# Levels 2 and 3, and level 4 and the pairs, of each head's chain as one run of small products each, from held copies; the sample's small products beside them

## The chip, the cores and the metric

The program runs on one core of a Trainium2 chip. Its time is the device time of one execution in microseconds (us). Before the change it is 2061.63 us, the median of three runs (2060.82 to 2062.42).

## The reference

One layer of a streaming encoder is computed for a prompt of 2048 tokens (width 1024) and for 32 further tokens of a running stream (the sample), with the same weights. Cut to what matters here:

```python
h = rmsnorm(x, g_pre_mix)
z = h @ w_in
u, zq, zf, zi, zg = jnp.split(z, [...], axis=-1)
y_pool = pool_mix(u_ext, n_valid, w_pool, pool_scale)
q = jax.nn.silu(zq)
fgate = lbf + (1.0 - lbf) * jax.nn.sigmoid(zff)
kin = (1.0 - lbf) * jax.nn.sigmoid(-zff)
logf = jnp.log(fgate)
S1, o = hgrn_run(S0, to_heads(q), to_heads(kin), to_heads(zi), to_heads(logf))
o = rmsnorm(o, g_hg_norm)
y_hg = o * jax.nn.silu(zg)
x = x + rmsnorm(jnp.concatenate([y_pool, y_hg], axis=-1) @ w_out, g_post_mix)
h2 = rmsnorm(x, g_pre_ffn)
x = x + rmsnorm((jax.nn.silu(h2 @ w_gate) * (h2 @ w_up)) @ w_down, g_post_ffn)
```

`hgrn_run` is a recurrence with a decay of its own for every token and channel, four heads of 128 channels. Within a chunk it needs, for every pair of tokens s <= t:

```python
b = jnp.cumsum(logf, axis=2)
decay = jnp.exp(jnp.where(causal, b[t] - b[s], -inf))
attn = jnp.einsum('bhtk,bhsk,bhtsk->bhts', q, k, decay)
o = attn @ v + (q * jnp.exp(b)) @ S0
S1 = jnp.exp(b_last) * S0 + (k * jnp.exp(b_last - b)).T @ v
```

## The kernel before, in words

**Stages.** The prompt is worked in two halves of 1024 tokens. The first half goes through the combined projection, the mixers, the output projection and the first part of the feed-forward layer, then the second half does the same, then the second feed-forward matrix follows for both. Almost all of TensorE's time is matmuls of 128x128 weights with 512 columns; each is done as three products of split numbers (a rounded part and its rest, float32r). In the second half of the prompt the projection runs in `front_pairs`, as seven products for each pair of column blocks, of 12 large matmuls each, whose weights (`wf`) are read from DRAM.

**The chain of a head.** Decays between two tokens are products of gates. The kernel builds them by levels: at level m tokens stand in blocks of 2^m. In a pair of neighbouring blocks the queries of the second are multiplied with the keys of the first, which gives the attention between the two; then the pair is merged: the keys of the first block are multiplied by the second block's total gate, the queries of the second by the first block's, and the totals by each other. `Levels.group` issues a level's products, `Levels.merge` a merge, with the keys on GpSimd (level 0 of the second half on VectorE) and queries and totals on VectorE. `pairs_of` writes into the spent gate tile `f_t` what level 1 needs, so that two kinds of queries go in one product with 32 columns. In `hgrn` a head of 1024 tokens has, per level, 32 matmuls of 32 keys with 16 queries (level 1: 32), each into its own 32 partitions of a PSUM bank; two banks (`gb`) hold levels 0 to 4 and the `pairs` (level 5, 16 matmuls), a third (`lv`) level 6. Each float32 matmul of this kind has two records in the profile. `hgrn` runs eight times, for four heads in each half; `sample_mix` does levels 0 to 4 for the sample, 4 matmuls each, into a bank `xgb`. So before the change a head has seven runs of small matmuls between the large ones: levels 0, 1, 2, 3, 4, pairs, 6.

**Order.** TensorE's order is the order in which the Python program calls `nc.tensor`, except that small work is put between the large matmuls: a `Task` is a generator that yields how many ns of TensorE work are to pass until its next piece, and after every third large matmul `poll` runs those that are due. `mm` counts the ns. A larger number in a `yield` moves the next piece back; the other engines and the DMA queue of SyncE are ordered by a scheduler that follows from it.

**Beside a group.** Tasks in `Pace.joint` (the sample's projections in the first half, `whole` in `sample_tile`, 8 matmuls of 32x128 each, into `fps`) are put right ahead of a level's group: `group` calls `join` first.

**PSUM.** Eight banks: four for the large products (`mmbank`) and four at the side (`axbank`), in turn, for gb, lv, xgb, kps (transposed keys), ups (state), ops2 (outputs), yps (outputs transposed back), and some others.

**Behind the levels.** Masks pick the attention out of gb (`masked`), keys are transposed (L1257), states updated (L1283), outputs summed (`ops2`), normalised in `out_stage` (ScalarE squares L1072, GpSimd L1073 and L1074, VectorE L1076), transposed back (`back`, L1083), multiplied by the gate (yr, L1303) and split (yhi, ylo). L206 is the matmul of the helper `mm`.

Of the kernel before, what the change touches and what calls it, by code (L numbers as in the profile page):

```python
# [16 lines left out]
P = 128  # L17
D = 1024
KD = D // P
NH = 4  # L20
# [11 lines left out]
STEP = 1900.0  # L32
# [9 lines left out]
NCH = HALF // CHUNK  # L42
# [42 lines left out]
def body(tc, ins, outs, cst):  # L85
    nc = tc.nc
    ctx = ExitStack()
    with ctx:
# [108 lines left out]
        class Pace:  # L197
            t = 0.0
# [6 lines left out]
        def mm(out, l, r, start, stop, ns, more=False):  # L205
            nc.tensor.matmul(out, l, r, start=start, stop=stop, skip_group_check=more)  # L206
            Pace.t += ns
# [606 lines left out]
        def sample_values():  # L814
            ws = []
            for k in range(KD):
                ws.append(t2("xwv"))
                nc.sync.dma_start(out=ws[k], in_=w_in[k * P:(k + 1) * P, COL_I:COL_I + 512])
                if k % 4 == 3:
                    yield 9000.0  # L820
                    if k == 3:
                        ps = axbank("vsps")
                    for kk in range(k - 3, k + 1):
                        sample_mm(ps, kk, KD, Smp.hsr[:, kk, :], ws[kk])
            Smp.vs = t2("vs")
            sample_sum(Smp.vs[0:NS], ps, 4)
# [24 lines left out]
        def join():  # L851

            for tk in Pace.joint:
                if not tk.begun:
                    tk.step()
            Pace.joint.clear()

        def use(S, kind, h, src, n0, n1):
            n = n1 - n0
# [149 lines left out]
        def half_of(L):  # L1009
            return lambda ap: ap.rearrange("p (a two l) -> p a two l", two=2, l=L)[:, :, 1, :]  # L1010

        class Levels:
# [2 lines left out]
            def __init__(self, n, k_t, qa, tt, place, blks):  # L1015
                self.n, self.k, self.qa, self.tt, self.place, self.blks, self.off = n, k_t, qa, tt, place, blks, 0

            def group(self, goff, src, pick, n=16):
                join()
                for c, j in self.blks:  # L1020
                    c0 = c * P + 32 * j
                    mm(self.place(c, j, goff, goff + n), self.k[:, c0:c0 + 32], pick(src[:, c0:c0 + 32]), True, True, 36.0)

            def merge(self, m, tcur, eng=nc.gpsimd):
                L = 1 << m
# [39 lines left out]
        def EVEN(ap):  # L1065
            return ap.rearrange("p (a two) -> p a two", two=2)[:, :, 0]
# [26 lines left out]
        def sample_mix():  # L1093

            z, v = Smp.z, nc.vector
            yield from sample_values()
            yield 3000.0
            s0 = t2("xs0", [P, NH, P])
            nc.sync.dma_start(out=s0, in_=ins["state_hgrn"][0, 0].rearrange("h k v -> k h v"))
            es = [t2("xes", [P, 4, 48]) for _ in range(3)]  # L1100
            nc.sync.dma_start(out=es[0][:, :, 0:HIST], in_=ins["cache_channels"].rearrange("(g p) t -> p g t", p=P))
            sg, w = t2("xsg", [P, 4, P]), t2("xw", [P, 4, P])
            nc.scalar.activation(sg[:, 0:3], z[:, 0:3], AF.Sigmoid)
            nc.scalar.activation(sg[:, 3], z[:, 0], AF.Sigmoid, scale=-1.0)
            f, k, q, qa = (w[:, i] for i in range(4))
            v.tensor_tensor(heads_of(f), heads_of(sg[:, 0]), by_head(oml), ALU.mult)
            v.tensor_tensor(heads_of(f), heads_of(f), by_head(lb), ALU.add)
            v.tensor_tensor(heads_of(k), heads_of(sg[:, 3]), by_head(oml), ALU.mult)
            v.tensor_tensor(q, z[:, 1], sg[:, 1], ALU.mult)
            v.scalar_tensor_tensor(sg[:, 2], z[:, 2], g_hg, sg[:, 2], ALU.mult, ALU.mult)  # L1110
            v.tensor_tensor(qa, q, f, ALU.mult)
            v.tensor_copy(es[0][:, :, HIST:HIST + NS], heads_of(z[:, 3]))
            vb, at, qb = t2("xvb"), t2("xat", [P, 4, P]), t2("xqb", [P, NH, P])
            rows, cm = at[:, 2], at[:, 3:4, 0:32]
            for tl in (vb, at, qb):
                nc.gpsimd.memset(tl, 0.0)
            for h in range(NH):
                r, hs = slice(32 * h, 32 * h + 32), slice(h * P, (h + 1) * P)
                v.tensor_scalar(rows[r], Smp.vs[0:NS, hs], Smp.rs[0:NS], None, ALU.mult)
                nc.gpsimd.tensor_copy(vb[r, hs], rows[r])  # L1120
            yield 14000.0
            for i in range(4):
                a, lev = (2 << i) - 1, 1 << i
                src, dst = (es[0] if i == 0 else es[1 + (i - 1) % 2]), es[1 + i % 2]
                n = HIST + NS
                v.tensor_tensor(dst[:, i:, a:n], src[:, i:, a:n], src[:, i:, a - lev:n - lev], ALU.add)
                v.scalar_tensor_tensor(Smp.ysr[:, i, :], dst[:, i, HIST:n], 1.0 / WINDOWS[i], es[0][:, i, HIST:n], ALU.mult, ALU.subtract)
            tail = small("tail", [P, 4, HIST], bufs=2)
            nc.gpsimd.tensor_copy(tail, es[0][:, :, NS:NS + HIST])
            gb = axbank("xgb")  # L1130
            L = Levels(P, k, qa, at[:, 1], lambda c, j, a, b: gb[32 * j:32 * j + 32, a:b], [(0, j) for j in range(4)])
            L.group(0, q, EVEN)
            yield 0.0
            tc_ = L.merge(0, f)
            L.pairs_of(f, q)
            yield 3000.0
            L.group(16, f, lambda ap: ap, 32)
            yield 0.0
            tc_ = L.merge(1, tc_)
            for m in (2, 3, 4):  # L1140
                yield 2000.0
                L.group(16 * (m + 1), qa, half_of(1 << m))
                yield 0.0
                tc_ = L.merge(m, tc_)
            masked(cm, lambda a, b: gb[:, a:b].unsqueeze(1), 0, 1, P)
            for h in range(NH):
                r = slice(32 * h, 32 * h + 32)
                nc.gpsimd.tensor_copy(at[r, 0, r], cm[r, 0])
                nc.gpsimd.tensor_copy(qb[:, h, r], qa[:, r])
            yield 6000.0  # L1150
            join()
            kps = axbank("kps")
            nc.tensor.transpose(kps[:, 0:P], k, ident)
            tick(107)
            kd = es[1].rearrange("p g t -> p (g t)")[:, 0:P]
            nc.scalar.copy(kd, kps[:, 0:P])
            pool_tail(outs[4], tail)
            yield 2500.0
            ops = axbank("ops2")
            mm(ops[:, 0:P], at[:, 0], rows, True, False, 218.0)  # L1160
            for h in range(NH):
                mm(ops[:, 0:P], qb[:, h], s0[:, h], False, h == NH - 1, 218.0)
            on = out_stage(ops, 1, P)
            ups = axbank("ups")
            mm(ups, kd, vb, True, True, 858.0)
            v.tensor_tensor(s0, s0, by_head(tc_, P), ALU.mult)
            v.tensor_tensor(s0, s0, ups.rearrange("p (h v) -> p h v", v=P), ALU.add)
            nc.sync.dma_start(out=outs[5][0, 0].rearrange("h k v -> k h v"), in_=s0)
            yield 4000.0
            yps = back(on, 1, P)  # L1170
            v.tensor_tensor(Smp.ysr[:, 4:8, :].rearrange("p h t -> p (h t)"), yps[:, 0:P], sg[:, 2], ALU.mult)
# [15 lines left out]
        def hgrn(S, H, h):  # L1187
            B = S.B
            f_t, k_t, q_t = H.f, H.k, H.q
# [5 lines left out]
            else:  # L1195
                vs = [t[:, h * P:(h + 1) * P] for t in S.vt]
            attn, cmp_ = S.attn, S.cmp
            qa = ztile("qa")
            nc.vector.tensor_tensor(qa, q_t, f_t, ALU.mult)
            gb = [axbank("gb") for _ in range(2)]  # L1200
            L = Levels(HALF, k_t, qa, ztile("tt"), lambda c, j, a, b: gb[c // 4][32 * j:32 * j + 32, c % 4 * 96 + a:c % 4 * 96 + b],
                       [(c, j) for c in range(NCH) for j in range(4)])
            L.group(0, q_t, EVEN)
            yield 0.0
            tc_ = L.merge(0, f_t, nc.vector if B else nc.gpsimd)
            if B:
                yield 2500.0
            L.pairs_of(f_t, q_t)
            yield 3000.0 if B else 5000.0
            L.group(16, f_t, lambda ap: ap, 32)  # L1210
            yield 0.0
            tc_ = L.merge(1, tc_)
            for m in (2, 3, 4):
                yield (STEP + 900.0 * (h + 1 == NH and m == 4)) if S.B else 1200.0 + 700.0 * (m == 3 and h + 1 < NH)
                L.group(16 * (m + 1), qa, half_of(1 << m))
                yield 0.0
                tc_ = L.merge(m, tc_)
            yield STEP + 900.0 * (S.B and h + 1 == NH)
            for c in range(NCH):
                o = 384 + c % 4 // 2 * 32  # L1220
                for j in (0, 2):
                    c0, q = c * P + 32 * j, 32 * (j + c % 2)
                    mm(gb[c // 4][q:q + 32, o:o + 32], k_t[:, c0:c0 + 32], qa[:, c0 + 32:c0 + 64], True, True, 55.0)
            yield 0.0
            tc_ = L.merge(5, tc_)
            yield STEP if S.B else 2800.0
            lv = axbank("lv")
            for c in range(NCH):
                q, o = c % 2 * 64, c // 2 * 64
# [3 lines left out]
            for sb in range(2):  # L1233
# [4 lines left out]
                for i in range(2):  # L1238
                    for j in (0, 2):
                        q = 32 * (j + i)  # L1240
# [875 lines left out]
```

## Time and profile before

| | before |
|---|---|
| median of three runs | 2061.63 us |
| the profiled execution's own time | 2061.65 us |
| its span (first to last instruction) | 2059.8 us |
| gb records on TensorE: levels 0 / 1 / 2 to 4 and pairs | 512 / 512 / 1792 |
| xgb records on TensorE | 40 |
| VectorE, ScalarE, GpSimd busy | 71%, 41%, 14% |

A row of a timeline is: start in us from the span's start, length in us, engine, line, operation, what it writes and reads, its form (for a matmul rows*columns of the array, then the size of the moving operand), count; in brackets idle time ahead of it and what ended it. A row of a table of waits is: who waited for whom, us in total, times, longest. A row of the groups by line ends with busy us, mean ns of one, idle us ahead of it and what ended that. Matmuls overlap, so starts say more than lengths.

### The profile page before, as it was taken

What the parts mean: (1) busy time and instruction counts of PE and PEld (TensorE: products, weight loads), DVE (VectorE), ACT (ScalarE), POOL (GpSimd) and SP (SyncE); (2) the same over time, 40 slices, a digit from 0 to 9 for tenths busy, and PEclk for the clock granted to TensorE, in tenths of its full rate; (3) what the DMA queues carried; (4) which work ended last, traced back from release to release, by engine and by line L of the source; (5) the groups of instructions that cost most, each with busy time, mean ns of one, the idle gap of its engine ahead of it and who ended that gap; (6) DMA issues with size and microseconds to landing.
All of it is one profiled execution on the core that took longest, in us unless ns stands there. A gap on an engine that the chain in (4) does not pass through costs nothing.

```text
span 2059.8 us, 34464 instructions
## 1 busy us (share of the span) xinstructions
PE 2047.2 (99%) x12980; PEld 1666.4 (81%) x12980; DVE 1455.6 (71%) x2322; ACT 851.9 (41%) x1689; POOL 293.1 (14%) x406
## 2 busy tenths in 40 slices
PE   9999999999999999999999999999999999999998
PEld 8788888888888888878888788888888778888876
DVE  5555574699877879676686697776676766566587
ACT  6544444654554544433444654444444521011032
POOL 0123332200000000033331200000000210110134
PEclk9999999999999999999999999999999999999999
DMA  8533343637777778756483614554445897776778
GB/s 293 197 107 114 104 143 123 195 98 230 239 227 231 222 220 269 232 177 207 137 293 119 203 43 132 168 155 143 143 140 167 245 345 214 213 226 202 217 205 219
DMA packets 431255, 389.14 MB, mean 189 GB/s; under 512 B 22360, under 2 KB 328528, under 8 KB 431088
## 3 DMA queue, kind: packets, MB, share of 16 engines
q1 hardware_dynamic: 424288, 376.65, 58.1%
q0 software_dynamic: 2144, 7.60, 1.9%
q10 hardware_dynamic: 4656, 2.67, 0.4%
q8 instruction: 103, 1.69, 0.3%
q14 instruction: 64, 0.52, 0.1%
HBM read 251.77 MB, written 135.07 MB: 188 GB/s over the span
## 4 chain that ended last, share of the span: by engine, by line
PE 92%; DVE 4%; ACT 1%; issue 1%; DMA 1%; POOL 1%; SPq 0%; DVEq 0%; POOLq 0%; ACTq 0%
PE gx L206 26%; PE gy L206 13%; PE dx L206 10%; PE ops L206 9%; PE mmb L206 8%; PE gz L206 6%; PE dy L206 5%; PE vps L206 4%; PE dz L206 3%; PE gb L206 1%; PE gw L206 1%; PE gsps L206 1%; DVE acc L1888 1%; PE tps L349 1%; PE ups L206 1%
## 5 line engine op out<-in xcount | busy, mean ns | idle before, releaser
L206 PE MATMUL gx<-fhi,wf 128*128 128x512 f32 x1632 | 462.7, 392 | 0.7 <-DMA wf<-wd 0.7
L206 PEld LDWEIGHTS gx<-fhi,wf 128*128 128x128 f32 x1632 | 303.6, 188 | 65.4 <-issue 3.3
L206 PE MATMUL gx<-flo,wf 128*128 128x512 f32 x816 | 255.1, 391 | 0.0
L206 PE MATMUL gy<-fhi,wf 128*128 128x512 f32 x832 | 240.1, 391 | 0.3 <-DVE c L1710 0.3
L206 PE MATMUL dx<-dhi,hst 128*128 128x512 f32 x640 | 185.4, 391 | 0.7 <-DVE acc L1888 0.6
L206 PEld LDWEIGHTS gy<-fhi,wf 128*128 128x128 f32 x832 | 155.3, 188 | 33.1 <-issue 1.1
L206 PEld LDWEIGHTS gx<-flo,wf 128*128 128x128 f32 x816 | 153.2, 188 | 32.0
L1888 DVE TENSOR_TENSOR acc<-dx,acc 128x512 f32<-128x512 f32 x168 | 115.1, 689 | 71.3 <-PE dx L206 70.2
L1604 DVE TENSOR_TENSOR wf<-s,wf 128x512 fp32r<-128x512 f32 x176 | 120.2, 687 | 53.8 <-ACT wf L1599 52.9
L206 PEld LDWEIGHTS dx<-dhi,hst 128*128 128x128 f32 x640 | 119.6, 188 | 30.0 <-issue 3.4
L1599 ACT CAST wf<-s 128x512 fp32r<-128x512 f32 x176 | 107.3, 620 | 62.0 <-PE gy L206 19.5
L206 PE MATMUL gy<-flo,wf 128*128 128x512 f32 x416 | 131.0, 392 | 0.0
L1827 ACT CAST dhi<-t 128x1024 fp32r<-128x1024 f32 x20 | 20.6, 1052 | 252.0 <-DVE dlo L1828 183.4
L1599 ACT CAST wf<-wraw 128x512 fp32r<-128x512 f32 x132 | 80.6, 621 | 80.3 <-PE gx L206 37.8
L206 PE MATMUL gz<-fhi,wf 128*128 128x512 f32 x384 | 112.4, 393 | 0.0
L1604 DVE TENSOR_TENSOR wf<-wraw,wf 128x512 fp32r<-128x512 f32 x132 | 89.6, 687 | 26.2 <-ACT wf L1599 26.0
L206 PE MATMUL dx<-dlo,hst 128*128 128x512 f32 x320 | 98.6, 389 | 0.0
L206 PE MATMUL dy<-dhi,hst 128*128 128x512 f32 x320 | 98.5, 389 | 0.0
L206 PEld LDWEIGHTS gy<-flo,wf 128*128 128x128 f32 x416 | 78.1, 188 | 16.9 <-issue 0.8
L206 PE MATMUL mmb<-hTlo,whi 128*128 128x512 f32 x256 | 90.2, 410 | 0.0
L1888 DVE TENSOR_TENSOR acc<-dy,acc 128x512 f32<-128x512 f32 x88 | 60.7, 689 | 38.4 <-PE dy L206 38.0
L1814 POOL TENSOR_TENSOR t<-wdr 128x1024 f32<-128x1024 f32 (+1 forms) x6 | 13.4, 2229 | 514.5 <-DVE hs L1519 405.6
(380 smaller groups left out, 4050.1 us busy)
## 6 DMA issues: line engine op xcount, KB each, us to landing
hst<-hdFalse SPq DMA_DIRECT2D x140, 256.0 KB, 3.0
hst<-hdTrue SPq DMA_DIRECT2D x140, 256.0 KB, 3.5
wf<-wd SPq DMA_DIRECT2D x112, 256.0 KB, 5.0
wraw<-in_w_gate_dram SPq DMA_DIRECT2D x50, 512.0 KB, 4.2
wraw<-in_w_up_dram SPq DMA_DIRECT2D x50, 512.0 KB, 4.2
hdFalse<-hhi SPq DMA_DIRECT2D x77, 256.0 KB, 2.7
hdFalse<-hlo SPq DMA_DIRECT2D x77, 256.0 KB, 2.9
hdTrue<-hhi SPq DMA_DIRECT2D x77, 256.0 KB, 2.3
```

The costliest lines, as they stand in the source:

```text
L206: nc.tensor.matmul(out, l, r, start=start, stop=stop, skip_group_check=more)
L349: nc.tensor.transpose(ps[:, c:c + P], xn[:, (2 * kp + kk) * P:(2 * kp + kk + 1) * P], ident)
L1599: nc.scalar.copy(wf[:, 0], getattr(M, src) if isinstance(src, str) else src)
L1604: nc.vector.tensor_tensor(wf[:, 1], getattr(M, src) if isinstance(src, str) else src, wf[:, 0].bitcast(F32), ALU.subtract)
L1814: nc.gpsimd.tensor_tensor(W.t1, b12, b11, ALU.subtract)
L1827: nc.scalar.copy(hi, src)
L1888: nc.vector.tensor_tensor(dst, ps, dst, ALU.add)
```

## The change

`hold` copies on ScalarE, ahead of the merges of levels 2 and 4, the keys and queries that the level's products need: the keys of the first blocks into `f_t` and the queries of the second blocks, packed, into `tt` (both were read for the last time). The merge then need not wait until TensorE has read them, and the level's products are issued behind the merge, in one run with those of the next level: 2 with 3, and 4 with the pairs. `steps` is now the order of the chain for heads and sample, with four delays. `group` no longer calls `join`; `steps` calls it at the start of each run, and for the sample it waits to be called itself: `meet` puts the sample's task into `Pace.joint`, so that its next piece is issued ahead of a head's run, or alone when its delay has passed (6000 ns; 4000 ns for the sample's value products).

```diff
@@ sample_values
-                    yield 9000.0
+                    yield 6000.0
+                    yield from meet(Smp.mix, 4000.0)
...
+        def meet(task, ns=6000.0):
+            task.begun = False
+            Pace.joint.append(task)
+            yield ns
+            task.begun = True
...
@@ class Levels
-            def group(self, goff, src, pick, n=16):
-                join()
+            def group(self, goff, pick, n=16, k=None):
+                k = self.k if k is None else k
                 for c, j in self.blks:
                     c0 = c * P + 32 * j
-                    mm(self.place(c, j, goff, goff + n), self.k[:, c0:c0 + 32], pick(src[:, c0:c0 + 32]), True, True, 36.0)
+                    mm(self.place(c, j, goff, goff + n), k[:, c0:c0 + 32], pick(c0), True, True, 36.0)
+
+            def hold(self, m, f):
+                n = self.n
+                fv, kv = (x[:, 0:n].rearrange("p (a two l) -> p a two l", two=2, l=1 << m)[:, :, 0, :] for x in (f, self.k))
+                nc.scalar.copy(fv, kv)
+                nc.scalar.copy(self.tt[:, 0:n // 2].rearrange("p (a l) -> p a l", l=1 << m), half_of(1 << m)(self.qa[:, 0:n]))
+
+            def steps(self, f, q, waits, eng0, last, start=lambda: (join(), ())[1]):
+                w0, w1, w2, w3 = waits
+                yield from start()
+                self.group(0, lambda c0: EVEN(q[:, c0:c0 + 32]))
+                yield 0.0
+                t = self.merge(0, f, eng0)
+                yield w0
+                self.pairs_of(f, q)
+                yield w1
+                yield from start()
+                self.group(16, lambda c0: f[:, c0:c0 + 32], 32)
+                yield 0.0
+                t = self.merge(1, t)
+                for m in (2, 4):
+                    yield w2
+                    self.hold(m, f)
+                    t = self.merge(m, t)
+                    yield w3
+                    yield from start()
+                    self.group(16 * (m + 1), lambda c0: self.tt[:, c0 // 2:c0 // 2 + 16], 16, f)
+                    if m == 2:
+                        self.group(64, lambda c0: half_of(8)(self.qa[:, c0:c0 + 32]))
+                    elif last is not None:
+                        last()
+                    yield 0.0
+                    if m == 2 or last is not None:
+                        t = self.merge(m + 1, t)
+                self.t = t
...
@@ sample_mix
-            for m in (2, 3, 4):
-                yield 2000.0
-                L.group(16 * (m + 1), qa, half_of(1 << m))
-                yield 0.0
-                tc_ = L.merge(m, tc_)
+            yield from L.steps(f, q, (0.0, 3000.0, 2000.0, 2000.0), nc.gpsimd, None, lambda: meet(Smp.mix))
+            tc_ = L.t
...
@@ hgrn
-            for m in (2, 3, 4):
-                yield (STEP + 900.0 * (h + 1 == NH and m == 4)) if S.B else 1200.0 + 700.0 * (m == 3 and h + 1 < NH)
-                L.group(16 * (m + 1), qa, half_of(1 << m))
-                yield 0.0
-                tc_ = L.merge(m, tc_)
-            yield STEP + 900.0 * (S.B and h + 1 == NH)
...
+            yield from L.steps(f_t, q_t, (1000.0, 4000.0, 1500.0, 2300.0) if B else (0.0, 5000.0, 1500.0, 2300.0),
+                               nc.vector if B else nc.gpsimd, pairs)
+            tc_ = L.t
```

How it moves instructions. On TensorE, in the first head of the first half (mmb are large products, wmp products that fold two weight matrices, fps the sample's projection, gb the levels; f_t and tt are the held copies); a piece of the difference, where level 2 from the copies and level 3 stand behind each other:

```order
+L206 MATMUL mmb<-hThi_439,whi 128x512
+L206 MATMUL mmb<-hThi_441,whi 128x512
+L206 MATMUL mmb<-hTlo_440,whi 128x512
 L206 MATMUL fps<-wraw,hsr 32x128 x8
+L206 MATMUL gb<-tt,f_t 32x16 x32
 L206 MATMUL gb<-qa,k_t 32x16 x32
+L206 MATMUL mmb<-hTlo_442,whi 128x512
+L206 MATMUL mmb<-hThi_439,wlo 128x512
+L206 MATMUL mmb<-hThi_441,wlo 128x512
```

Before, only one gb group stood between two large products here; the other one stood elsewhere. In the same way level 4 (`gb<-tt,f_t 32x16 x32`) is now followed by the pairs (`gb<-qa,k_t 32x32 x16`), in each of the eight heads.

On TensorE in the second half, before: the levels of the sample (xgb) between the large products gx of the first head's chain:

```order
L206 MATMUL gb<-qa,k_t 32x16 x32
L206 MATMUL gx<-fhi,wf 128x512 x2
L206 MATMUL gx<-flo,wf 128x512
L206 MATMUL xgb<-xw 32x16 x4
L206 MATMUL gx<-flo,wf 128x512
L206 MATMUL gx<-fhi,wf 128x512 x4
L206 MATMUL gx<-flo,wf 128x512 x2
L206 MATMUL gx<-fhi,wf 128x512 x2
L206 MATMUL gb<-qa,k_t 32x16 x32
```

And now, at the start of the second head's chain, ahead of the first head's outputs transposed back (yps), of which a second group of four follows the last row; the held group `xgb<-xat,xw 32x16 x4` stands just ahead of the first row:

```order
L206 MATMUL xgb<-xw 32x16 x4
L206 MATMUL gb<-q_t,k_t 32x16 x32
L206 MATMUL gx<-flo,wf 128x512
L206 MATMUL gx<-fhi,wf 128x512 x2
L206 MATMUL gz<-fhi,wf 128x512 x2
L206 MATMUL gz<-flo,wf 128x512 x2
L206 MATMUL gz<-fhi,wf 128x512 x4
L206 MATMUL gz<-flo,wf 128x512
L1128 MATMUL yps<-cons,on 128x128 x4
L206 MATMUL gz<-flo,wf 128x512
L206 MATMUL gz<-fhi,wf 128x512 x2
```

The sample's levels 2 and 3 moved from the first head's chain to the second head's first run, so xgb is still in use when yps is written; its level 4 follows in the second head's second run.

On VectorE at that place now, from the first head's normalised outputs (on) to their reading from yps (yr):

```order
L1121 TENSOR_TENSOR on<-ops_9440,ost 128x512
L1079 TENSOR_TENSOR xw<-xw,xat 128x4x16
L1080 TENSOR_TENSOR tt<-tt 128x64
L1080 TENSOR_TENSOR tt<-tt 128x32
L1080 TENSOR_TENSOR tt<-tt 128x16
L1080 TENSOR_TENSOR tt<-tt 128x8
L1079 TENSOR_TENSOR qa<-qa,tt 128x256x2
L1325 TENSOR_TENSOR yr<-yps,g_t 128x512
```

Merges of the second head and of the sample stand between the two; before, the second head's gates, its qa, its first tt and its first merge stood there.

More of the change, by code (lines that the diff above doesn't have):

```diff
@@ L1131, in sample_mix @@
             L = Levels(P, k, qa, at[:, 1], lambda c, j, a, b: gb[32 * j:32 * j + 32, a:b], [(0, j) for j in range(4)])
-            L.group(0, q, EVEN)
-            yield 0.0
[L1134 to L1137, printed above, removed]
-            yield 0.0
-            tc_ = L.merge(1, tc_)
-            for m in (2, 3, 4):
-                yield 2000.0
-                L.group(16 * (m + 1), qa, half_of(1 << m))
-                yield 0.0
-                tc_ = L.merge(m, tc_)
+            yield from L.steps(f, q, (0.0, 3000.0, 2000.0, 2000.0), nc.gpsimd, None, lambda: meet(Smp.mix))
+            tc_ = L.t
             masked(cm, lambda a, b: gb[:, a:b].unsqueeze(1), 0, 1, P)
@@ L1202, in hgrn, with pairs @@
                        [(c, j) for c in range(NCH) for j in range(4)])
[L1203 to L1212, printed above, removed]
-            for m in (2, 3, 4):
-                yield (STEP + 900.0 * (h + 1 == NH and m == 4)) if S.B else 1200.0 + 700.0 * (m == 3 and h + 1 < NH)
-                L.group(16 * (m + 1), qa, half_of(1 << m))
-                yield 0.0
-                tc_ = L.merge(m, tc_)
-            yield STEP + 900.0 * (S.B and h + 1 == NH)
[L1219 to L1225, printed above, removed]
+            def pairs():
+                for c in range(NCH):
+                    o = 384 + c % 4 // 2 * 32
+                    for j in (0, 2):
+                        c0, q = c * P + 32 * j, 32 * (j + c % 2)
+                        mm(gb[c // 4][q:q + 32, o:o + 32], k_t[:, c0:c0 + 32], qa[:, c0 + 32:c0 + 64], True, True, 55.0)
+            yield from L.steps(f_t, q_t, (1000.0, 4000.0, 1500.0, 2300.0) if B else (0.0, 5000.0, 1500.0, 2300.0),
+                               nc.vector if B else nc.gpsimd, pairs)
+            tc_ = L.t
             yield STEP if S.B else 2800.0
```

## The prediction

> **What bounds the kernel now.** I read the page's engine table and chain first, then TensorE's waits, then its timeline around the small products that the change moves. The page, in two of its parts:
>
> ```profile
> PE 2047.2 (99%) x12980; PEld 1666.4 (81%) x12980; DVE 1455.6 (71%) x2322; ACT 851.9 (41%) x1689; POOL 293.1 (14%) x406
> ```
>
> ```profile
> PE 92%; DVE 4%; ACT 1%; issue 1%; DMA 1%; POOL 1%; SPq 0%; DVEq 0%; POOLq 0%; ACTq 0%
> ```
>
> TensorE is busy for 99% of the span, and 92% of the chain that ended last runs through it. All that it waited for, in the view of TensorE's waits:
>
> ```profile
> PE idle L206 <- POOL ones L149: 1.0, 1, 1.0
> PE yps L1083 <- DVE on L1076: 0.9, 1, 0.9
> PE gx L206 <- DMA wf<-wd: 0.7, 1, 0.7
> PE dx L206 <- DVE acc L1888: 0.6, 2, 0.4
> PE gb L206 <- ACT xz L845: 0.4, 1, 0.4
> PE gy L206 <- DVE c L1710: 0.3, 1, 0.3
> ```
>
> That is 3.9 us in seven waits. So the time is the sum of what TensorE executes, and every other engine has slack until it makes TensorE wait. The change is worth what it takes out of that sum, less new waits.
>
> **What a run of small products costs.** The change removes no matmul. It only lets small ones follow each other that were split by 128x512 matmuls, so I need the price of a run's entry and exit. The timeline (start, length, form, count of records) first gives the pace of the large ones where no small one intervenes:
>
> ```profile
> 104.61 0.63 PE L206 MATMUL mmb<-hTlo,whi 128*128 128x512 f32 x2
> ...
> 106.91 0.61 PE L206 MATMUL mmb<-hThi,whi 128*128 128x512 f32 x2
> ```
>
> Ten starts in 2.30 us (the three rows left out are equal pairs): 0.23 us each. Then a level's group alone:
>
> ```profile
> 87.63 0.62 PE L206 MATMUL mmb<-hThi,wlo 128*128 128x512 f32 x2
> 88.19 0.73 PE L206 MATMUL gb<-qa,k_t 128*32 128x16 f32 x64
> 88.85 0.73 PE L206 MATMUL mmb<-hThi,whi 128*128 128x512 f32 x2
> 89.42 0.40 PE L206 MATMUL mmb<-hTlo,whi 128*128 128x512 f32 x1
> ```
>
> A projection group of the sample alone:
>
> ```profile
> 260.56 0.39 PE L206 MATMUL mmb<-hTlo,whi 128*128 128x512 f32 x1
> 260.88 0.64 PE L206 MATMUL fps<-wraw,hsr 128*32 128x128 f32 x16
> 261.45 0.50 PE L206 MATMUL mmb<-hTlo,whi 128*128 128x512 f32 x1
> 261.79 0.64 PE L206 MATMUL mmb<-hThi,wlo 128*128 128x512 f32 x2
> ```
>
> Both behind each other:
>
> ```profile
> 76.50 0.63 PE L206 MATMUL mmb<-hThi,wlo 128*128 128x512 f32 x2
> 77.06 0.65 PE L206 MATMUL fps<-wraw,hsr 128*32 128x128 f32 x16
> 77.52 0.76 PE L206 MATMUL gb<-q_t,k_t 128*32 128x16 f32 x64
> 78.21 0.73 PE L206 MATMUL mmb<-hThi,whi 128*128 128x512 f32 x2
> 78.78 0.62 PE L206 MATMUL mmb<-hTlo,whi 128*128 128x512 f32 x2
> ```
>
> And two projection groups behind each other:
>
> ```profile
> 63.53 0.61 PE L206 MATMUL mmb<-hThi,wlo 128*128 128x512 f32 x2
> 64.08 1.08 PE L206 MATMUL fps<-wraw,hsr 128*32 128x128 f32 x32
> 65.09 0.73 PE L206 MATMUL mmb<-hThi,whi 128*128 128x512 f32 x2
> 65.66 0.62 PE L206 MATMUL mmb<-hTlo,whi 128*128 128x512 f32 x2
> ```
>
> From the start of the large row ahead to the start of the row after the next large one, less 0.23 us for each large matmul within: gb alone 1.79 - 4 x 0.23 = 0.87 us; fps alone 1.23 - 2 x 0.23 = 0.77; both in one run 2.28 - 0.92 = 1.36; two fps groups in one run 2.13 - 0.92 = 1.21. Joined, the pair costs 1.36 instead of 1.64, and the two fps 1.21 instead of 1.54. **A join of two such groups saves 0.28 to 0.33 us**; I take 0.30. All of these have the form 128*32, in which four groups of 32 columns work beside each other, as have gb, xgb and vsps; only joins among these are counted.
>
> The trace of before has no join of a level with a level, so I bound it. From above, 0.33. From below, what the last matmul of a run alone takes to drain:
>
> ```profile
> L206 PE MATMUL gb<-qa,k_t x1792: 179/183/217, 88.2 to 1043.2; 128*32 128x16 f32 x171, 128*32 128x32 f32 x29
> ```
>
> 0.18 us (the median). A join that saves less, or costs, I exclude for this form: the joined rows above save more.
>
> The Trainium skill has a rule for this, "TensorE: Matmul & The Clock Gate", Part 3 (Packing small matmuls): tiles packed side by side take one matmul's duration and some 4 ns for each further tile. By that rule a join saves one duration only, and the sum below would be smaller by 2.4 us. This trace does not bear the rule out for a run's length: it gives 0.44 us for 64 records, where the rows above show 0.87.
>
> **The change, part by part.**
>
> *Joins in the heads.* Before, levels 2, 3, 4 and the pairs of each head are four runs. Now there are two: level 2 from the held copies with level 3, and level 4 from the held copies with the pairs. Eight heads, two joins each: 16 x 0.30 = 4.8 us.
>
> *Joins of the sample.* Its five level groups (xgb) ran alone before. In TensorE's new order one of them rides with a head's level 4, two (levels 2 and 3) stand ahead of another head's first group, one ahead of that head's second, and one stays alone: four joins, 1.2 us. The vsps runs are one joined and one alone as before. The fps groups stand beside a level's group eight times in either order, so they bring nothing.
>
> *Held copies.* Each head adds four copies on ScalarE (keys and queries, before the merges of levels 2 and 4), the sample four small ones. Their nearest rows and that of the merge:
>
> ```profile
> L1043 ACT COPY f_t<-q_t 128x512 f32<-128x512 f32 x8 | 5.3, 661 | 12.2 <-DVE tt L1035 7.2 <-POOL k_t L1033 2.9 <-DVE k_t L1033 2.2
> ...
> L1033 POOL TENSOR_TENSOR k_t<-k_t,tt 128x512 f32<-128x512 f32 x48 | 67.6, 1408 | 99.9 <-PE gb L206 61.3 <-issue 12.9 <-DVE wlo L250 5.9
> ```
>
> 32 x 0.66 = 21 us of ScalarE, which is 41% busy: no cost by itself. But a run now follows two merges and a copy: 1.41 + 0.66 + 1.41 = 3.5 us, and with the hand-overs between engines I put it at 4.0. In TensorE's new order 24 large matmuls (24 x 0.23 = 5.5 us) stand between a head's runs in most heads, in the others 15 to 21 with other small runs among them, which comes to about the same. Cover is some 1.5 us, and 0.7 more for the merged keys, which only the second group of a run reads. I count nothing; if the cover is gone, each late microsecond is a wait of TensorE.
>
> *A PSUM bank that is held longer.* The sample's levels now end a head later. So when the first head of the second half transposes its result back (yps, two groups of four), the four side banks hold the next head's two gb banks, xgb and the first yps; the second yps must wait until VectorE has read the first. In the trace of before:
>
> ```profile
> 930.22 0.39 PE L206 MATMUL ops<-S,qa 128*128 128x128 f32 x2
> ...
> 933.71 0.69 DVE L1076 TENSOR_TENSOR on<-ops,ost 128x512 f32<-128x512 f32 x1 [1.96 <-POOL ost L1074]
> ...
> 943.10 0.86 DVE L1035 TENSOR_TENSOR tt<-tt 128x64 f32<-128x64 f32 x4
> ```
>
> Of the groups by line:
>
> ```profile
> L1034 DVE TENSOR_TENSOR qa<-qa,tt 128x512 f32<-128x512 f32 x48 | 39.6, 825 | 16.9 <-PE gb L206 14.4 <-PE lv L206 1.9 <-ACT f_t L1043 0.2
> ...
> L1303 DVE TENSOR_TENSOR yr<-yps,g_t 128x512 f32<-128x512 f32 x16 | 10.6, 683 | 0.1
> ```
>
> The normalised result is ready at 934.40, 3.8 us after the last output product ends (930.61). In VectorE's new order come behind it a merge of the sample (64 columns, put at 0.3), the four small tt (0.86), a merge of qa (0.83) and then yr (0.68): 2.7 us, so the bank is free 6.5 us behind the products. TensorE gets there after 18 large matmuls (4.1 us), the joined run (0.87, with two groups of the sample 1.0) and the first yps (put at 0.5): 5.6 us. A new wait of 0.9 us; bounds 0 and 1.5.
>
> *Old waits.* The gb wait of 0.4 us is the third head's second group, which waited for the copies of the pairs. In the new order that group stands 0.7 us of large matmuls later, and no reduction of the second half's statistics stands between the copies: it goes. The yps wait of 0.9 at the end of the last head has the same distance to its products in both orders; I leave it, and the other four.
>
> **The sum.** The profiled execution took 2061.65 us (span 2059.8 and 1.85 around it), 0.02 above the median of the three. 2061.65 - 4.8 - 1.2 + 0.9 - 0.4 = **2056.15, say 2056.2 us**.
>
> **Rivals.**
>
> *A join saves only the drain.* Then 20 x 0.18 = 3.6 us: 2061.65 - 3.6 + 0.9 - 0.4 = 2058.55. For it: that drain is in every row; here a group with other weights (the held keys, then the merged ones) follows. Against it: both joins of the trace change weights too and save 0.28 and 0.33. This is the time by the rule of the Trainium skill above. Chance 0.15.
>
> *Held copies late in some heads.* Where two yhi casts and two sigmoids stand ahead of the copies on ScalarE (the second head of the second half; 4 x 0.66 = 2.6 us if each is as long as a copy), the cover of 1.5 us is short by 1.1; three such heads with one late run each cost 3.3 us: 2059.5. Against it: the casts read a result that is there before the merge of the keys is. Chance 0.09.
>
> *Slower.* The same mechanism in every run: ScalarE takes its instructions in order, and whatever stands ahead of a held copy delays merge and run. It decides from 0.6 us late per run (16 x 0.6 = 9.6, against 5.5 gained and 4.1 for the bound); with 1.0 us in all 16 the time is 2072.2. Against it: TensorE's waits for ScalarE are 0.4 us in all now. Chance 0.04.
>
> That the change does not do what it says, TensorE's order excludes: all 16 joins stand in it.
>
> **How the numbers follow.** Forecast 0.72, the rivals 0.15, 0.09 and 0.04. The low end has 0.33 a join, no new wait and the yps wait gone as well: 2061.65 - 6.6 - 0.4 - 0.9 = 2053.75, say 2053.8; the high end takes in the first two rivals: 2059.5. Outside lie the last rival and what I have not seen, under 2 in 10. A measurement can tell 0.2% (4.1 us) from no change, so faster is below 2057.5: most of the forecast, 0.70. Within: the rest of it and two rivals, 0.26. Slower 0.04.
>
> **What would show it.** In the new timeline a run of 64 gb<-tt and 64 gb<-qa records should cost 1.41 to 1.46 us by the same reckoning (1.56 if only the drain is saved), and 64 with 32 some 0.3 less. The waits should show yps behind yr, under 1.5 us, no gb behind ScalarE, and an unchanged rest. A gb run that waits for f_t, tt or k_t would show the second or third rival; waits of over 5 us in all would make the forecast wrong.

## The result and the profile after

| | before | after |
|---|---|---|
| median | 2062.51 us (2060.82 to 2064.10, 12 runs) | 2058.06 us (2057.33 to 2058.49, 12 runs) |
| ratio of the two | | 0.9979, 95% interval 0.9970 to 0.9988 |
| the profiled execution: its time, its span | 2061.65, 2059.8 us | 2058.00, 2055.4 us |

The change makes the kernel 4.4 us faster (0.21%). The forecast had 5.5 us less, and the time lies in its range (2053.8 to 2059.5). The two profiled executions differ by 4.4 us in span but by 3.65 us in time, since 1.85 us lie around the span before and 2.6 us after.

The page of the kernel after, its engine table:

```profile
PE 2041.4 (99%) x12980; PEld 1668.8 (81%) x12980; DVE 1447.6 (70%) x2322; ACT 869.7 (42%) x1725; POOL 283.7 (14%) x406
```

TensorE still bounds the kernel, busy for 99% of the span. Its busy time fell by 5.8 us (2047.2 to 2041.4). What is left of the span, its idle time, rose from 2059.8 - 2047.2 = 12.6 to 2055.4 - 2041.4 = 14.0 us. So 5.8 us went out of the work and 1.4 came back as waiting. Counted in the two timelines, the runs of small products of the form 128*32 fell from 61 to 41: the twenty joins that were forecast, at 5.8 / 20 = 0.29 us each. ScalarE's 36 more instructions are 18 us more of its time.

A joined run in the timeline after (level 2 from the held copies, then level 3):

```profile
196.23 0.62 PE L206 MATMUL mmb<-hThi,wlo 128*128 128x512 f32 x2
196.78 0.74 PE L206 MATMUL gb<-tt,f_t 128*32 128x16 f32 x64
197.38 0.73 PE L206 MATMUL gb<-qa,k_t 128*32 128x16 f32 x64
...
198.60 0.62 PE L206 MATMUL mmb<-hTlo,whi 128*128 128x512 f32 x2
```

By the prediction's reckoning: 2.37 - 4 x 0.23 = 1.45 us for 128 records (the row left out is an equal pair). A level with the pairs, and ahead of it a group of the sample:

```profile
898.91 0.61 PE L206 MATMUL gx<-flo,wf 128*128 128x512 f32 x2
...
899.91 0.26 PE L206 MATMUL xgb<-xw 128*32 128x16 f32 x8
899.99 0.75 PE L206 MATMUL gb<-tt,f_t 128*32 128x16 f32 x64
...
901.55 0.63 PE L206 MATMUL gz<-flo,wf 128*128 128x512 f32 x2
```

Left out are a large pair ahead of the run and one behind it, and the 32 records of the pairs. From 898.91 to 901.55 stand six large matmuls: 2.64 - 6 x 0.23 = 1.26 us for 104 records. The sample's 8 records start 0.08 us ahead of the level and cost little more than that.

TensorE's waits in the profile after:

```profile
PE idle L206 <- POOL ones L149: 1.1, 1, 1.1
PE ops L206 <- DVE S L1303: 1.1, 1, 1.1
PE lv L206 <- DVE qa L1079: 0.8, 2, 0.5
PE yps L1128 <- DVE yr L1325: 0.8, 1, 0.8
PE dx L206 <- DVE acc L1910: 0.7, 2, 0.4
PE tps L349 <- ACT h2raw L358: 0.4, 1, 0.4
PE vps L206 <- ACT xg L678: 0.4, 1, 0.4
PE gy L206 <- DVE c L1732: 0.3, 1, 0.3
PE yps L1128 <- DVE on L1121: 0.3, 1, 0.3
```

They are 5.9 us in all, against 3.9 before. No gb waits any more, so the held copies are in time in all runs. The wait of yps for yr is the one that was forecast. The waits of ops for S and of lv for qa are new and were not forecast; nor were three small ones, of tps, of vps and of the first yps for its result (on). Gone are the waits of gb for xz (0.4, forecast), of yps for the last head's result (0.9) and of gx for its weights (0.7); the last two were not forecast, and why they went was not tried.

Where the first of the two new waits comes from, in the timeline of TensorE and VectorE after, at the last head of the first half:

```profile
267.75 0.61 PE L206 MATMUL ups<-va,kd 128*128 128x128 f32 x4
...
272.56 0.49 PE L206 MATMUL ops<-S,qa 128*128 128x128 f32 x2 [1.05 <-DVE S L1303]
```

```profile
268.49 0.19 DVE L1368 TENSOR_TENSOR eh<-eh 128x30 f32<-128x30 f32 x1 [1.36 <-POOL eh L1361]
268.59 1.22 DVE L1367 TENSOR_TENSOR sb<-sa 128x1021 f32<-128x1021 f32 x1
...
271.10 1.21 DVE L1371 SCALAR_TENSOR_TENSOR sb<-sa,e_t 128x1008 f32<-128x1008 f32 x1
272.22 0.28 DVE L1303 COPY S<-ups 128x128 f32<-128x128 f32 x1
```

VectorE works through a pooling window before it copies the first state (shown are a small instruction that waits for GpSimd, and then the first and the last of three of 1.2 us; left out are the middle one and small ones). The products `ups` that it copies had started at 267.75. In the timeline of before, VectorE at the same place, the copy and then the start of that window:

```profile
266.36 0.29 DVE L1281 COPY S<-ups 128x128 f32<-128x128 f32 x1 [0.48 <-PE ups L206]
...
271.73 1.23 DVE L1345 TENSOR_TENSOR sa<-e_t 128x1023 f32<-128x1023 f32 x1 [0.58 <-ACT e_t L862]
```

So it is not the data of the copy that is late but VectorE's order: the copy stood ahead of this chain and waited for `ups` alone, now it stands behind it. Inside the chain VectorE stood idle for 1.36 us until GpSimd had made its piece of the window (eh), longer than the 1.05 us that TensorE waited. So a wait of VectorE for a third engine is part of this price; no run takes it out by itself.

The second, at the third head of the second half (lv starts at 988.71, after 0.53 us of waiting for the last qa shown here):

```profile
985.20 0.69 DVE L1009 TENSOR_TENSOR ylo<-yr,yhi 128x512 fp32r<-128x512 f32 x1
985.81 1.55 DVE L882 SCALAR_TENSOR_TENSOR g_t<-c,cons,sg 128x512 f32<-128x512 f32 x1
987.28 0.68 DVE L1325 TENSOR_TENSOR yr<-yps,g_t 128x512 f32<-128x512 f32 x1
987.88 0.68 DVE L1079 TENSOR_TENSOR qa<-qa,tt 128x512 f32<-128x512 f32 x1
```

A head's chain is shorter by two runs now. On VectorE its last merge stands behind the tail of the head before (yr, ylo), which has not become shorter, and behind a gate's product (g_t, 1.55 us, the longest of the four rows).

### The profile page after: what moved, and what is told of

Its sections match the earlier page's. It is cut to its first block, busy times and chain, and to the rows that moved or that the text cites. A ratio compares the mean times of both kernels' runs of the same rounds, so it can differ in the third digit from the quotient of the medians.

```text
span 2055.4 us, 34455 instructions
## 1 busy us (share of the span) xinstructions
PE 2041.4 (99%) x12980; PEld 1668.8 (81%) x12980; DVE 1447.6 (70%) x2322; ACT 869.7 (42%) x1725; POOL 283.7 (14%) x406
## 4 chain that ended last, share of the span: by engine, by line
PE 92%; DVE 4%; POOL 1%; DMA 1%; issue 1%; ACT 1%; SPq 0%; DVEq 0%; ACTq 0%; POOLq 0%
PE gx L206 26%; PE gy L206 13%; PE dx L206 10%; PE ops L206 10%; PE mmb L206 8%; PE gz L206 6%; PE dy L206 5%; PE vps L206 4%; PE dz L206 3%; PE gw L206 1%; PE gb L206 1%; PE gsps L206 1%; DVE acc L1910 1%; PE ups L206 1%; PE tps L349 1%
```

## The experiments

Each ratio is against the kernel before, timed beside it.

**1. The joined groups taken apart again.**

```diff
-                    yield w3
+                    yield w3 - 700.0 * (last is not None)
...
                     if m == 2:
+                        if last is not None:
+                            yield 700.0
                         self.group(64, ...)
                     elif last is not None:
+                        yield 700.0
                         last()
```

> The held copies stay; between the two groups of each of the 16 joined runs of the heads some three large matmuls are put back (the first group is issued earlier by as much, so that the second keeps its place). Theory (the joins carry the gain): 64 with 64 records should cost 0.85 + 0.85 us apart instead of 1.45, 64 with 32 0.85 + 0.58 instead of 1.18; 16 x 0.25 = 4.0 us back, so about the time of the kernel before the change (ratio 0.9995 to 1.0005), and 16 more runs of small products in the timeline. Rival 1 (a join saves only the drain of a last matmul, 0.18): 2.9 us back. Rival 2 (the gain is from waits that moved, not from joins): the time of the change within 0.5 us, ratio near 0.998.

Measured: 2064.75 us, ratio 1.0009 (1.0000 to 1.0017), so some 6.2 us above the change (0.0030 of the time). In its timeline the two groups (left out are three large matmuls between them and one behind):

```profile
980.14 0.63 PE L206 MATMUL gy<-fhi,wf 128*128 128x512 f32 x2
980.70 0.74 PE L206 MATMUL gb<-tt,f_t 128*32 128x16 f32 x64
...
982.25 0.74 PE L206 MATMUL gb<-qa,k_t 128*32 128x16 f32 x64
...
983.26 0.62 PE L206 MATMUL gy<-fhi,wf 128*128 128x512 f32 x2
```

3.12 - 6 x 0.23 = 1.74 us for the two groups, against 1.45 joined: **0.29 us a join** here, 16 x 0.29 = 4.6 in all. By time, rival 2 falls (the ratio is not that of the change), and by these rows rival 1 falls too (0.18 a join). The count of runs of the form 128*32 is 57, 16 more than in the change. The span of the profiled execution is 7.1 us above that of the change; what the joins leave over is a longer wait and what followed it:

```profile
994.86 0.86 PE L206 MATMUL lv<-qa,k_t 128*64 128x64 f32 x16 [2.27 <-DVE qa L1082]
...
996.24 1.91 PE L206 MATMUL gz<-fhi,wf 128*128 128x512 f32 x4
...
999.18 0.62 PE L206 MATMUL gx<-fhi,wf 128*128 128x512 f32 x2
```

lv waits 2.3 us in one place instead of 0.8 in two. Behind it the granted clock is 0.50 from 996 to 998 us of this profile, and TensorE takes 4.3 us from the start of lv to the last row shown, where the same work takes 2.8 us in the change: 1.5 us more. TensorE's busy time is 5.7 us above that of the change (2047.1 against 2041.4); without this stretch it is 4.2, or 0.26 a join, so 0.29 for each of the 16 is a little high. The slow stretch does not follow from every such wait: in experiment 4 lv waits 2.25 us, and the large matmuls behind it keep their pace. The wait of ops for S is there as well (1.1 us), so it hangs on the changed order, not on the joins.

**2. Two of the new waits, a first attempt.** The last head of the first half goes through its transposes earlier, and a spilled head's second transpose back comes later:

```diff
-            yield 1000.0 if S.B else 500.0 + 2500.0 * (h + 1 == NH)
+            yield 1000.0 if S.B else 500.0 + 500.0 * (h + 1 == NH)
...
                     put_y(S, 4 + h, cols, yr)
-                yield 500.0
+                yield 1700.0 if spill else 500.0
```

> Two delays changed: the transposes and state products of the last head of the first half come 2.0 us earlier, and in the second half the second transpose back of a head that is spilled comes 1.2 us later. Theory (the wait of 1.1 us of ops for S is VectorE's order: the copy of the first state stands behind a chain of the pooling window; and the wait of 0.8 us of yps for yr is the PSUM bank): both waits go, less than 0.3 us is left of each, and the time falls by 1.5 to 1.9 us below that of the change (ratio 0.9970 to 0.9973). Rival (the waits only move to the next instruction that needs VectorE): the same total of TensorE's waits, 6.1 us, and a ratio of 0.998.

Measured: 2058.68 us, ratio 0.9983 (0.9974 to 0.9992): no gain. TensorE's waits:

```profile
PE ops L206 <- DVE S L1303: 1.1, 1, 1.1
...
PE ops L206 <- DVE S L1305: 0.8, 1, 0.8
```

The PSUM half of the theory held: the wait of yps for yr is no longer in the list. The other half failed. Asking earlier brought the state copy ahead of the last instruction of the pooling window on VectorE, but not ahead of the window; the same wait stood there, a second one behind it, and the transposes (kps) now waited 0.6 us for GpSimd's merge. (Its profile also loses 1.9 us against that of the change at the start of the program, see the last section.)

**3. and 7. How much cover the held copies have.** Each copy made three times, and twice:

```diff
-                    self.hold(m, f)
+                    for _ in range(3):
+                        self.hold(m, f)
```

> Each held copy is made three times over, so each of the 16 runs of the heads has four copies more ahead of it on ScalarE, 4 x 0.62 = 2.5 us. Prediction's cover (1.5 us between what a run needs and what it has): each run is about 1.0 us late, TensorE waits for gb on ScalarE, VectorE or GpSimd for up to 16 x 1.0 = 16 us in all. Rival (the cover is over 2.5 us, because ScalarE is idle and runs ahead): no gb in TensorE's waits, and the time of the change within 1 us.

Measured, one run: 2067.55 us. The first of five rows in which gb waits:

```profile
PE gb L206 <- DVE qa L1080: 2.8, 6, 0.7
```

The five are 6.7 us in all: eleven waits of gb, in ten of the 16 runs, where the prediction's cover would have given up to 16 us and the rival nothing. Ten of the eleven stand ahead of a run's second group, which needs the merge behind the copies; only one waits for a copy itself (tt, 1.0 us). So the cover is shorter than 2.5 us in most runs, and longer than the 1.5 us that I had put in most. The rest of the time lost lies elsewhere, 1.9 us of it at the start of the program and 1.0 in a wait of ups for ScalarE.

> Each held copy made twice: 2 x 0.62 = 1.25 us more ahead of each of the 16 runs. With three copies (2.5 us more) 12 of 16 runs were late, by 0.55 us on average and 1.7 at most, which puts the cover of the change at 2.5 - 0.55, about 2 us, with one run at 0.8. Theory: at 1.25 us more only that one run (the second head from the end, its run of 64 with 64) is late, by 0.4 us; all gb waits together under 0.8 us. Rival (the prediction's cover of 1.5 us everywhere): none late. Rival (late copies are paid through ScalarE's other work, not through the runs): other waits for ScalarE appear, 1 us or more.

Measured, one run: 2059.02 us. Its longest wait:

```profile
PE ops L206 <- DVE S L1304: 1.9, 1, 1.9
```

One gb run is late, by 0.6 us (0.4 expected, at the run named). But ops waits 0.8 us longer for VectorE than in the change, and lv 1.4 us in one place. That the copies cause this is not shown: no wait for ScalarE is in the list, and with three copies the wait of ops for S is not there at all.

**4. The sample issued by its own timers.**

```diff
-                    yield 6000.0
-                    yield from meet(Smp.mix, 4000.0)
+                    yield 9000.0
...
-            yield from L.steps(f, q, (0.0, 3000.0, 2000.0, 2000.0), nc.gpsimd, None, lambda: meet(Smp.mix))
+            yield from L.steps(f, q, (0.0, 3000.0, 2000.0, 2000.0), nc.gpsimd, None)
```

> The sample's groups and its values are issued by their own timers as before the change; the heads keep their joined runs. Theory: five xgb runs of 0.38 to 0.40 us each alone, so 1.2 us of joins are lost; the sample's levels end within the first head of the second half, so the bank is free and the wait of yps for yr (0.8 us) is gone; the heads' runs of 64 with 64 records stay at 1.45. Rival (the bank is held by the heads' own gb and not by the sample): the yps wait stays at 0.8 us or so.

Measured, one run: 2058.84 us. No yps behind yr is in the list of its waits any more. In its timeline the second group of yps starts while VectorE still reads the first:

```profile
935.34 0.69 DVE L1324 TENSOR_TENSOR yr<-yps,g_t 128x512 f32<-128x512 f32 x1
935.55 0.60 PE L1127 MATMUL yps<-cons,on 128*128 128x128 f32 x4
```

So the bank was held by the sample, as the theory has it. Of the sample's four joins only two were lost: its levels 2 and 3 still stood side by side, and another of its groups fell beside a head's level by chance; busy time is only 0.2 us above that of the change. So this run settles the bank, and not the price of the sample's joins. In it lv waits 2.3 us in one head, as in experiment 1: this wait changes with the order.

**5. The output products later.** The transposes stay as in the change; `ops` of that head comes later (and the second transpose back as in experiment 2):

```diff
-            yield 5500.0 if B else 1200.0 + 1600.0 * (h + 1 == NH)
+            yield 5500.0 if B else 1200.0 + 3600.0 * (h + 1 == NH)
```

> Two delays changed against the change: the last head of the first half issues its output products 2.0 us later (its transposes stay), and in the second half the second transpose back of a spilled head comes 1.2 us later. Theory (VectorE's order: the first state is there 1.1 us after the output products ask for it, and was not there earlier either when everything was moved up by 2.0 us in the run before; so the products must move back, not the transposes up): ops behind S is gone or under 0.2 us, yps behind yr under 0.2, TensorE's waits fall from 6.1 to about 4.3 us and the time by 1.8 us, ratio near 0.997. Rival (the output products are needed where they are; the end of the first half waits instead): a new wait of 1 us or more between 270 and 300 us, and no gain.

Measured: 2055.52 us, ratio 0.9969 (0.9957 to 0.9981), span 2052.8. All of TensorE's waits:

```profile
PE idle L206 <- POOL ones L149: 1.1, 1, 1.1
PE lv L206 <- DVE qa L1079: 0.8, 2, 0.5
PE tps L349 <- ACT h2raw L358: 0.8, 1, 0.8
PE dx L206 <- DVE acc L1910: 0.7, 2, 0.4
PE yps L1128 <- DVE on L1121: 0.3, 1, 0.3
```

3.7 us instead of 5.9: both waits are gone (1.05 and 0.79 us), and nothing took their place between 270 and 300 us. The span is 2.6 us shorter, of which 0.6 lies in the first 10 us of the program, where the edit changes nothing (see the last section). The ratio is 0.0010 lower (2.1 us); its interval overlaps that of the change, so it is the trace that says where the gain is. VectorE's order is the cause of the one wait and the PSUM bank of the other, and nearly all of the gain is theirs.

**6. lv later as well**, on top of experiment 5's two delays.

```diff
-            yield STEP if S.B else 2800.0
+            yield STEP + 800.0 * (h > 1) if S.B else 2800.0
...
-            yield 1000.0 if S.B else 500.0 + 2500.0 * (h + 1 == NH)
+            yield 1000.0 - 800.0 * (h > 1) if S.B else 500.0 + 2500.0 * (h + 1 == NH)
```

> As the run before it in this call, and in the last two heads of the second half the level-6 products (lv) stand 0.8 us later, with 0.8 us less behind them. Theory (lv reached VectorE's queue ahead of its merge because the head's chain is shorter now, and meets the tail of the head before): lv behind qa (0.8 us in two waits) is gone, kps behind it stays free (it had 3.6 us), and the time is 0.8 us below that of the run before. Rival (the wait moves on to kps or to the end of the last head): the sum of TensorE's waits stays the same.

Measured: 2058.20 us, ratio 0.9982 (0.9973 to 0.9991), 2.7 us above experiment 5. The theory failed; the rival had the direction, but the waits grew instead of staying the same (5.9 us against 3.7):

```profile
PE yps L1128 <- DVE on L1121: 1.0, 2, 0.7
...
PE kps L1279 <- POOL k_t L1078: 0.6, 1, 0.6
```

lv no longer waits, but kps does, and so does yps at the end of the last head, and ops and gx wait 0.4 us each. (1.0 us of the 5.9 is a wait at the start of the program, which this edit does not touch.) Here a wait inside a chain whose end is awaited could not be delayed away.

**8. Two more joins.**

```diff
-            task = Task(whole(), 6500.0 if h or kind > 1 else 14000.0)
+            task = Task(whole(), 9500.0 if h or kind > 1 else 14000.0)
```

> On top of the run with the later output products: a projection group of the sample waits up to 9.5 us instead of 6.5 for a level's group to join, so in the order two more of the 13 join (both the level-0 group of a later head). Theory (a join of fps with a level saves 0.28): 2 x 0.28 = 0.56 us less in the runs, which cost 1.35 to 1.43 joined against 0.77 + 0.86 alone, and a time of 2054.9, ratio 0.9966. Rival (the weights are held longer, so their loads come later): a wait on a load or on VectorE of 0.5 us or more, and nothing gained.

Measured: 2055.24 us, ratio 0.9967 (0.9957 to 0.9978). By time it can't be told from experiment 5; by the trace it can. Without the edit (the timeline of experiment 5), and with it:

```profile
176.62 0.62 PE L206 MATMUL mmb<-hThi,whi 128*128 128x512 f32 x2
...
179.65 0.64 PE L206 MATMUL fps<-wraw,hsr 128*32 128x128 f32 x16
...
181.11 0.74 PE L206 MATMUL gb<-q_t,k_t 128*32 128x16 f32 x64
...
182.81 0.62 PE L206 MATMUL mmb<-hThi,wlo 128*128 128x512 f32 x2
```

```profile
176.64 0.62 PE L206 MATMUL mmb<-hThi,whi 128*128 128x512 f32 x2
...
180.36 0.64 PE L206 MATMUL fps<-wraw,hsr 128*32 128x128 f32 x16
180.82 0.76 PE L206 MATMUL gb<-q_t,k_t 128*32 128x16 f32 x64
...
182.54 0.62 PE L206 MATMUL mmb<-hThi,wlo 128*128 128x512 f32 x2
```

Between the first and the last row of each stand the same matmuls, 16 of them large. They take 6.19 us apart and 5.90 joined: 0.29 us a join again. No wait for the weights appeared. This version has the lowest median of all that ran, by less than the runs can tell.

## Why the prediction was right, and by what it was off

- **What bounds the kernel:** right. TensorE is busy for 99% of the span after as before, and its work and its waits account for the change of the span.
- **The joins, 6.0 us:** nearly right. Busy time fell by 5.8. The joined runs cost 1.45 us, within the 1.41 to 1.46 that was to be seen, and a join 0.29 us by the rows of experiments 1 and 8 (0.26 by the busy time of experiment 1), where 0.30 was taken. The rival "only the drain" would have shown 1.56 us; it falls with the same rows. The prediction also reached that rival's time by a rule of the Trainium skill ("TensorE: Matmul & The Clock Gate", Part 3, Packing small matmuls), whose table there ends at 16 tiles; carrying it on to 64 records was the prediction's own step, and the 0.87 us that it had for such a run already spoke against it. What the fixed share of a run consists of, no run here shows.
- **Held copies at no cost:** right in the change. The cover was put too short (1.5 us); experiment 3 leaves ten of 16 runs late, by 0.67 us on average, at 2.5 us more. The two rivals of late copies did not come.
- **The PSUM bank, 0.9 us:** right, 0.8, and by the reason given: it goes without the sample (experiment 4) and with 1.2 us more between the two transposes (2 and 5). The sum for it left out that the first yps itself waits 0.3 us there for its result.
- **The old gb wait, 0.4 us:** gone, as predicted.
- **"I leave it, and the other four":** this is the step that failed. Two of the old waits that were left in the sum went (0.9 of yps and 0.7 of gx), and new ones came for which the sum had no term: ops for S 1.1, lv for qa 0.8, tps 0.4, vps 0.4, and yps for on 0.3. TensorE's idle time rose by 1.4 us where +0.9 - 0.4 = +0.5 was forecast (the listed waits rose by 2.0; the difference lies in gaps too small for the list). That is 0.9 of the 1.1 us by which the span's gain (4.4) missed the forecast one (5.5); the other 0.2 is the joins. About half of the 0.9 is not the change's: the wait of vps at the start of the program is absent before and in experiments 5 and 7, and 0.3 to 1.1 us in the other profiles.

The prediction named a sign that would make its forecast wrong, waits of over 5 us in all. They are 5.9, and the time lies in the range all the same, because the busy time fell as forecast and because two waits happened to go. That is luck: with these two still there the time would be some 1.6 us longer, 2059.7 us by an estimate from the median and their 0.9 and 0.7, just outside the range. The chance of 0.70 stood on a time below 2057.5 us, which the median of 2058.06 did not reach.

The method of that step was at fault more than its size. The prediction looked for places where TensorE's order changes, and drew up VectorE's order for one of them only, the transposes back (yps); both larger new waits come from where VectorE's instructions ended up at other places. For the first of them the length of the window's instructions, 1.2 us each, could be read in the trace of before; whether that would have given the wait was not tried.

## What to carry to other kernels

Here a run of small products among large ones costs a fixed share (about 0.3 us) and then a price for each record (0.009 us, from 0.87 us for 64 and 1.45 for 128), so putting two runs together pays that share once, if the operands can be held. When a chain gets shorter, list for every engine what its instructions now stand behind, and not only for the engine that bounds: the largest of the new waits came from VectorE's order. Here such a wait was mended by asking later where nothing else then waited (experiment 5, 2 us for two numbers), and not by asking earlier (2) or by delaying a chain whose end is awaited (6).

## What the runs showed that was not expected

At the start of the program the same matmuls take different times from one profiled execution to the next. The timeline of the change, and then of experiment 2, behind the first wait:

```profile
6.29 1.65 PE L206 MATMUL vps<-whw,xg 128*128 128x512 f32 x6 [0.40 <-ACT xg L678]
```

```profile
6.55 2.93 PE L206 MATMUL vps<-whw,xg 128*128 128x512 f32 x6 [0.82 <-ACT xg L678]
```

By the starts of these rows and of the ones behind them (7.78 and 9.28), six matmuls take 1.49 us in one (0.25 each) and 2.73 in the other (0.46 each), though the granted clock reads 1.00 in every microsecond of both from 4 to 12 us. The Trainium skill ("TensorE: Matmul & The Clock Gate", Part 1, The HAM clock gate) has a start at half rate whose length changes from run to run. These rows agree with that; the granted clock, which fell to 0.50 in the slow stretch of experiment 1, does not show it here, so the cause stays open. It is 1.2 us on these rows alone, over a quarter of what this change brings.

So profiles of this kernel are better compared behind the start. The first row of a single vps matmul with wlw starts at 8.65 us before the change, at 9.16 after it, at 11.09 in experiment 2 and at 8.60 in experiment 5. From there to the end the span of the change is 4.9 us shorter than that of before, where the whole span says 4.4 and the forecast was 5.5.
